# Feed-forward networks in two halves of inner features, with nine of 22 blocks as seven products of quarters

## The chip, the cores and the metric

One core of a Trainium2 chip runs the whole program. Its engines work side by side, each through its own queue in order: TensorE (PE, with its weight loads shown as PEld), VectorE (DVE), ScalarE (ACT), GpSimd (POOL) and SyncE (SP), which issues nearly all transfers. The metric is the device time of one execution in microseconds (us); lower is better.

## The reference, cut to what matters

The program runs a small sequence model: 512 tokens of 1,024 features pass two blocks with a mixer and two feed-forward networks each, and then further mixers on a longer sequence. The change touches the four feed-forward networks of the first part. Each computes, with 2,816 inner features:

```
def rmsnorm(x, g, eps=NORM_EPS):
    x32 = x.astype(jnp.float32)
    y = x32 * lax.rsqrt(jnp.mean(x32 * x32, axis=-1, keepdims=True) + eps)
    return (y * g.astype(jnp.float32)).astype(x.dtype)

def swiglu(h, w_up, w_down):
    gate, up = jnp.split(h @ w_up, 2, axis=-1)
    return (jax.nn.silu(gate) * up) @ w_down
```

and half of the result is added to x. All of it is in fp32.

## The kernel before, in words

**Layout.** Features lie on the 128 partitions and the 512 tokens along the free axis, so x is 8 tiles of 128x512 and the inner features are 22 blocks of 128. Block j has a gate and an up block of weights; each is one piece of 128x1024 (8 chunks of 128x128, half a megabyte) that SP fetches by one transfer.

**fp32 by three products.** TensorE takes each fp32 operand as two fp32r numbers, a high and a low part. `split` makes them: ScalarE copies the high part (L212), VectorE subtracts it from the source (L215; L206 and L209 are its forms with a scale or a bias). `mm3` (L227 to L231) then issues three matmuls, high x high, low x high and high x low. A gate or up block is 8 chunks x 3 = 24 matmuls of 512 columns, a pair 48. `weights` (L217) holds three buffers for a raw piece (`wraw`) and three pairs for its parts (`whi`, `wlo`). `bank` gives out four PSUM banks (`mm`).

**One network** (`ffn_body`, L318). The high and low parts of x are `hh` and `hl`, 8 tiles each. The reciprocal root of the mean square (`rbc`, copied from PSUM by L302) comes during the first pair. For each of 22 blocks j: 48 matmuls into two banks; VectorE multiplies the gate by `rbc` (L337), ScalarE takes silu (L338), VectorE multiplies up by `rbc` (L339), multiplies both (L340), and `split` leaves the result as `ah`, `al` (one pair of tiles for each j). Then the down projection: for each of 8 output blocks 22 chunks of weights in three pieces (1024, 1024 and 768 columns), 66 matmuls, and L346 adds half of the result to x.

**Work that is threaded through.** `extra` is a generator; `next(extra)` runs one step of it after each pair and after each down block, 30 times a network. The first two networks have none. The third carries `modulation(0)`, 24 steps: a step fetches a piece of `mod_w` into a `wraw` buffer and accumulates two halves of it, on VectorE into `acc` (L780), on ScalarE and GpSimd into `sq` (L781, L782); every fourth step ends an output of the modulation (two splits, four matmuls L792, L795, transposes, L799). The fourth network carries `context_in` (5 steps, 256-column work, tiles `ci`) and then `modulation(1)` (24 steps). After the fourth network `first_out` squares the 8 tiles of x on ScalarE (L727) and sums them on VectorE (L724, L728, L729) in the tiles `acc`, `sq` and `rbc`; `acc` and `sq` have one buffer each and are the same tiles as in modulation. The matmuls L262 with `ones` follow from its `acc`, and nothing of the next layer's normalised input exists before them. The next mixer's `ci` matmuls do not need them.

**Order.** A scheduling layer orders each engine's queue from the program text and puts in the semaphore waits; the queues then run in that fixed order.

## Time and profile before

| | |
|---|---|
| median of 3 runs | 3098.17 us (3096.71 to 3101.39) |
| the profiled execution | 3100.21 us, span 3098.5 us |
| TensorE busy | 3021.2 us, 98% |
| TensorE weight loads | 2519.9 us, 81% |
| VectorE busy | 1952.0 us, 63% |
| ScalarE busy | 1343.7 us, 43% |
| GpSimd busy | 451.6 us, 15% |
| granted TensorE clock | 9 tenths or more in each of 40 slices |

The span is what the program takes between its first and last instruction; the 1.7 us between it and the profiled time lie around it. Busy shares are means over the whole program, in which the four networks take about 1,460 us (60 to 422, 584 to 943, 943 to 1313 and 1640 to 2010 us).

### The profile page before, as it was taken

How to read it: one execution, taken by the hardware profiler on the slowest of the kernel's cores; microseconds unless marked ns; L12 is line 12 of the kernel's file. 1: busy time of each engine (PE TensorE's matmuls, PEld its weight loads, DVE VectorE, ACT ScalarE, POOL GpSimd, SP SyncE). 2: the span in 40 equal slices, each digit the busy share in tenths (PEclk: the TensorE clock that was granted, in tenths of full speed). 3: DMA queues.
4: the chain of work that ended last, by engine and by line, in shares of the span. 5: the costliest groups of instructions: out<-in, count | busy, mean ns of one | idle time of the engine just before them, and what ended most of it. 6: DMA issues, size and time to landing. Idle time of an engine off the chain costs nothing. (4 is left out here: it accounts for less than half of the span.)

```text
span 3098.5 us, 39749 instructions
## 1 busy us (share of the span) xinstructions
PE 3021.2 (98%) x15210; PEld 2519.9 (81%) x15210; DVE 1952.0 (63%) x3051; ACT 1343.7 (43%) x2359; POOL 451.6 (15%) x300
## 2 busy tenths in 40 slices
PE   8999999999999999999999999999999999999998
PEld 7888888888888888878788888878888887987776
DVE  6444357444436665377747665488778887668885
ACT  5332234322224443345535443346545643456663
POOL 0000000000002221023300221114334430001110
PEclk9999999999999999999999999999999999999999
DMA  6333322333334444312133444434344434531112
GB/s 205 95 97 92 100 86 78 101 96 100 92 100 130 132 148 127 98 56 62 54 88 124 136 143 133 146 96 137 111 125 147 137 111 156 173 103 38 37 54 92
DMA packets 112927, 335.84 MB, mean 108 GB/s; under 512 B 13512, under 2 KB 22984, under 8 KB 112736
## 3 DMA queue, kind: packets, MB, share of 16 engines
q1 hardware_dynamic: 112736, 333.30, 34.8%
q8 instruction: 119, 1.95, 0.3%
q14 instruction: 72, 0.59, 0.1%
HBM read 321.25 MB, written 11.96 MB: 108 GB/s over the span
## 5 line engine op out<-in xcount | busy, mean ns | idle before, releaser
L229 PE MATMUL mm<-hh,whi 128*128 128x512 f32 x2312 | 913.7, 395 | 6.5 <-DVE bt L1085 2.8
L230 PE MATMUL mm<-hl,whi 128*128 128x512 f32 x2312 | 905.1, 391 | 0.5 <-DVE hl L209 0.5
L231 PE MATMUL mm<-hh,wlo 128*128 128x512 f32 x2312 | 904.9, 391 | 0.0
L212 ACT ACTIVATE whi<-wraw 128x1024 fp32r<-128x1024 f32 (+3 forms) x458 | 462.0, 1012 | 953.0 <-PE mm L230 638.0
L215 DVE TENSOR_TENSOR wlo<-wraw,whi 128x1024 fp32r<-128x1024 f32 (+3 forms) x413 | 496.5, 1203 | 312.2 <-ACT whi L212 307.0
L229 PEld LDWEIGHTS mm<-hh,whi 128*128 128x128 f32 x2312 | 435.3, 188 | 96.7 <-DVE bt L1085 3.2
L231 PEld LDWEIGHTS mm<-hh,wlo 128*128 128x128 f32 x2312 | 435.5, 188 | 91.7 <-issue 1.0
L230 PEld LDWEIGHTS mm<-hl,whi 128*128 128x128 f32 x2312 | 435.5, 188 | 85.5 <-DVE hl L209 0.9
L229 PE MATMUL mm<-ah,whi 128*128 128x512 f32 x704 | 274.2, 390 | 0.0
L231 PE MATMUL mm<-ah,wlo 128*128 128x512 f32 x704 | 273.9, 389 | 0.0
L230 PE MATMUL mm<-al,whi 128*128 128x512 f32 x704 | 273.9, 389 | 0.0
L215 POOL TENSOR_TENSOR wlo<-wraw,whi 128x1024 fp32r<-128x1024 f32 (+1 forms) x69 | 168.7, 2445 | 393.6 <-ACT whi L212 246.0
L782 POOL TENSOR_TENSOR sq<-sq,wraw 128x512 f32<-128x512 f32 x84 | 122.3, 1456 | 437.3 <-ACT wraw L781 432.3
L339 DVE TENSOR_TENSOR fu<-mm,rbc 128x512 f32<-128x512 f32 x88 | 60.6, 689 | 185.8 <-PE mm L231 185.6
L229 PE MATMUL mm<-ci,whi 128*128 128x256 f32 (+1 forms) x552 | 166.5, 303 | 11.0 <-DVE bt L1085 5.0
L266 POOL TENSOR_TENSOR rs_r<-rs_v,neghalf 128x4 f32<-128x4 f32 (+1 forms) x23 | 25.4, 1104 | 1038.2 <-DVE rs_v L265 1038.2
L231 PE MATMUL mm<-ci,wlo 128*128 128x256 f32 (+1 forms) x552 | 164.6, 298 | 0.7 <-POOL wlo L215 0.7
L229 PEld LDWEIGHTS mm<-ah,whi 128*128 128x128 f32 x704 | 132.1, 188 | 27.6
L230 PEld LDWEIGHTS mm<-al,whi 128*128 128x128 f32 x704 | 132.1, 188 | 27.5
L231 PEld LDWEIGHTS mm<-ah,wlo 128*128 128x128 f32 x704 | 132.1, 188 | 27.5
L1197 ACT ACTIVATE lb<-lb,nbias 128x128 f32<-128x128 f32 x384 | 119.7, 392 | 35.1 <-POOL lb L1194 35.0
L230 PE MATMUL mm<-ci,whi 128*128 128x256 f32 x464 | 134.7, 290 | 0.0
(500 smaller groups left out, 4741.9 us busy)
## 6 DMA issues: line engine op xcount, KB each, us to landing
wraw<-w_up SPq DMA_DIRECT2D x176, 512.0 KB
wraw<-w_down SPq DMA_DIRECT2D x64, 512.0 KB
wraw<-mod_w SPq DMA_DIRECT2D x48, 512.0 KB
wraw<-m_in SPq DMA_DIRECT2D x48, 512.0 KB
lb<-cum_scr SPq DMA_DIRECT2D x64, 384.0 KB
wraw<-w_down SPq DMA_DIRECT2D x32, 384.0 KB
wraw<-diff_qkv SPq DMA_DIRECT2D x24, 512.0 KB
el<-ecum_scr SPq DMA_DIRECT2D x64, 192.0 KB
```

The lines of the kernel that those rows point to most:

```text
L212: nc.scalar.activation(hi, src, AF.Copy)
L215: (rest or nc.vector).tensor_tensor(lo, src, hv, op=ALU.subtract)
L229: mm(ps, ah, bh, start=start, stop=False)
L230: mm(ps, ah, bl, start=False, stop=False)
L231: self.last_mm = mm(ps, al, bh, start=False, stop=stop)
L266: nc.gpsimd.tensor_tensor(r[:, :nb], v[:, :nb], self.neghalf[:, :nb], op=ALU.pow)
L339: nc.vector.tensor_tensor(u, pu, rbc(), op=ALU.mult)
L782: nc.gpsimd.tensor_tensor(acc[1], acc[1], w, op=ALU.add)
L1197: nc.scalar.activation(w[dr][:, c], w[dr][:, c], AF.Exp, bias=nbias[:, c, dr * 32 + h : dr * 32 + h + 1])
```

## The change

The inner features are taken in two halves of 11 blocks: only 11 pairs `ah`, `al` are kept, and the down projection runs twice, each time over 11 chunks (pieces of 1024 and 384 columns) with an addition to x (L360 of the changed kernel). That frees the room for sums of the input. In every second block from j = 4 (4, 6, ... 20; nine in a network, 36 in all) the pair is done by `ffn_seven`. It views weights and input as 2 x 2 quarters (gate and up by two halves of the input features; input features by two halves of the tokens) and forms seven products of quarters, each 4 chunks x 3 = 12 matmuls of 256 columns: 84 matmuls of 256 columns in place of 48 of 512. For it VectorE makes four combinations of weight quarters (L396, L397, L400, L403) and their low parts (three of 1024 columns, one of 512), and puts the products together in seven operations of 256 columns (L425 to L437), followed by two multiplications by `rbc` of 512 (L434, L438). `ffn_sums` makes the four sums of input quarters, a quarter of them in each of the first four blocks: 4 operations of 256 columns (L375 to L378), and 4 splits of 256 columns. `next(extra)` is called in the 13 ordinary blocks and in the 16 passes of the down projection: 29 times a network. The fourth network's extra work has 29 steps, so its last step now runs behind the last pass of the down projection.

```diff
+            a2 = [(fp.tile([P, S], F32R, name=f"ah{j}"), fp.tile([P, S], F32R, name=f"al{j}")) for j in range(n)]
...
             for j in range(NFF):
...
+                t = u = None
+                if j >= 4 and j % 2 == 0:
+                    t, u = self.ffn_seven(fp, up[2 * j], up[2 * j + 1], hh, hl, sums, rbc)
+                else:
+                    pg, pu = self.bank(), self.bank()
+                    self.dense(up[2 * j], [(pg, hh, hl)])
+                    self.dense(up[2 * j + 1], [(pu, hh, hl)], within=rbc.start if j == 0 else None)
...
+                    next(extra, None)
                 nc.vector.tensor_tensor(u, t, u, op=ALU.mult)
-                self.split(u, ah[j], al[j])
-                next(extra, None)
-            for m in range(KC):
-                ps = self.bank()
-                self.dense(down[m], [(ps, ah, al)])
-                nc.vector.scalar_tensor_tensor(self.x[m], ps, 0.5, self.x[m], op0=ALU.mult, op1=ALU.add)
-                next(extra, None)
+                self.split(u, ah[j % n], al[j % n])
+                if j < 4:
+                    self.ffn_sums(fp, j, g, sums)
+                if j % n == n - 1:
+                    at = (j // n) * n * P
+                    for m in range(KC):
+                        ps = self.bank()
+                        self.dense(down[m][:, at : at + n * P], [(ps, ah, al)])
+                        nc.vector.scalar_tensor_tensor(self.x[m], ps, 0.5, self.x[m], op0=ALU.mult, op1=ALU.add)
+                        next(extra, None)
...
+        y = fp.tile([P, S], F32, name="fg", bufs=2)
+        nc.scalar.activation(y, z, AF.Copy, scale=gz)
+        w = fp.tile([P, S], F32, name="fu", bufs=2)
+        nc.vector.scalar_tensor_tensor(w[:, h0], x[:, h1], gx, y[:, h1], op0=ALU.mult, op1=ALU.add)
+        nc.vector.scalar_tensor_tensor(w[:, h1], x[:, h0], gx, w[:, h0], op0=ALU.mult, op1=ALU.subtract)
+        nc.vector.tensor_tensor(y[:, h0], y[:, h0], w[:, h1], op=ALU.add)
+        nc.vector.tensor_tensor(y[:, h1], x[:, h0], x[:, h1], op=ALU.subtract)
+        for q, (src, scale) in enumerate(((w[:, h0], None), (w[:, h1], -1.0), (y[:, h1], gx), (y[:, h0], None))):
+            self.split(src, sums[q][c][:, h0], sums[q][c][:, h1], scale=scale)
...
+        gh, gl = pair()
+        self.split(wg, gh, gl)
+
+        nc.vector.tensor_tensor(wt[:, b1], wu[:, b0], wg[:, b0], op=ALU.subtract)
+        nc.vector.tensor_tensor(wt[:, b0], wu[:, b1], wt[:, b1], op=ALU.subtract)
+        th, tl = pair()
+        self.split(wt, th, tl)
+        nc.vector.tensor_tensor(wu[:, b0], wu[:, b1], wu[:, b0], op=ALU.subtract)
+        uh, ul = pair()
+        self.split(wu, uh, ul)
+        nc.vector.tensor_tensor(wg[:, b1], wt[:, b0], wg[:, b1], op=ALU.subtract)
...
+        product(pa[:, h0], gh, gl, 0, quarter(0, h0))
+        nc.scalar.activation(v[:, h0], pa[:, h0], AF.Copy)
+        product(pb[:, h0], th, tl, 0, total(1))
+        product(pa[:, h1], gh, gl, 512, quarter(4, h0))
+        tt(t[:, h0], pa[:, h1], v[:, h0], op=ALU.add)
+        tt(v[:, h0], pb[:, h0], v[:, h0], op=ALU.add)
+        product(pc[:, h0], th, tl, 512, total(0))
+        tt(v[:, h1], pc[:, h0], v[:, h0], op=ALU.add)
+        product(pb[:, h1], uh, ul, 0, total(2))
+        tt(v[:, h0], pb[:, h1], v[:, h0], op=ALU.add)
+        tt(u[:, h1], pc[:, h0], v[:, h0], op=ALU.add)
+        product(pc[:, h1], vh, vl, 0, quarter(4, h1))
+        tt(t[:, h1], v[:, h0], pc[:, h1], op=ALU.subtract)
+        tt(t, t, r, op=ALU.mult)
+        nc.scalar.activation(t, t, AF.Silu)
+        product(pd[:, h0], uh, ul, 512, total(3))
+        tt(u[:, h0], pd[:, h0], v[:, h1], op=ALU.add)
+        tt(u, u, r, op=ALU.mult)
```

The scheduling layer's order decides what stands ahead of what. Three places of VectorE's queue follow. The first is in the third network, where pairs run with modulation's steps (L780 before, L869 in the changed kernel). Before, an ordinary block reads:

```order
L339 TENSOR_TENSOR fu<-mm,rbc 128x512
L780 SCALAR_TENSOR_TENSOR acc<-wraw,silu_c,acc 128x512
L340 TENSOR_TENSOR fu<-fg,fu 128x512
L215 TENSOR_TENSOR wlo<-wraw,whi 128x1024
L215 TENSOR_TENSOR al_6768<-fu,ah_6746 128x512
L780 SCALAR_TENSOR_TENSOR acc<-wraw,silu_c,acc 128x512
L337 TENSOR_TENSOR fg<-mm,rbc 128x512
L215 TENSOR_TENSOR wlo<-wraw,whi 128x1024
```

In the changed kernel a block of seven products has there the operations that put products together, between the low parts of the next weights:

```order
L425 TENSOR_TENSOR fg<-mm,fv 128x256
L426 TENSOR_TENSOR fv<-mm,fv 128x256
L215 TENSOR_TENSOR wlo<-wraw,whi 128x1024
L428 TENSOR_TENSOR fv<-mm,fv 128x256
L215 TENSOR_TENSOR wlo<-wraw,whi 128x1024
L430 TENSOR_TENSOR fv<-mm,fv 128x256
L869 SCALAR_TENSOR_TENSOR acc<-wraw,silu_c,acc 128x512
L431 TENSOR_TENSOR fu<-mm,fv 128x256
L437 TENSOR_TENSOR fu<-mm,fv 128x256
L869 SCALAR_TENSOR_TENSOR acc<-wraw,silu_c,acc 128x512
L438 TENSOR_TENSOR fu<-fu,rbc 128x512
```

L431 stands behind two low parts, L428, L430 and one step of modulation. The matmuls of the product `pc[:, h1]`, which write the bank that L431 reads, wait for it; on TensorE they stand among the first matmuls of the next block.

The second place is the start of the third network, block j = 2, where the changed kernel has:

```order
L215 TENSOR_TENSOR wlo<-wraw,whi 128x1024 x2
L349 TENSOR_TENSOR fu<-mm,rbc 128x512
L375 SCALAR_TENSOR_TENSOR fu<-x_92,cols,fg 128x256
L351 TENSOR_TENSOR fu<-fg,fu 128x512
L376 SCALAR_TENSOR_TENSOR fu<-x_92,cols,fu 128x256
L378 TENSOR_TENSOR fg<-x_92 128x256
L377 TENSOR_TENSOR fg<-fg,fu 128x256
L215 TENSOR_TENSOR al_8058<-fu,ah_8057 128x512
L215 TENSOR_TENSOR s_8077<-fu,s_8077 128x256
L206 SCALAR_TENSOR_TENSOR s_8081<-fu,s_8081 128x256
L206 SCALAR_TENSOR_TENSOR s_8085<-fg,cols,s_8085 128x256
L215 TENSOR_TENSOR s_8089<-fg,s_8089 128x256
```

The eight rows of 128x256 (L375 to L378, and the four splits into tiles s) are new in this block and stand between the ordinary ones.

The third place is the end of the fourth network. Before, VectorE has the sixth of the eight additions to x, the end of modulation (L795, L799), and then the first sums of squares:

```order
L346 SCALAR_TENSOR_TENSOR x_96<-mm,x_96 128x512
L215 TENSOR_TENSOR wlo<-wraw,whi 128x1024
L795 TENSOR_TENSOR acc<-aux,sq 2x512
L215 TENSOR_TENSOR wlo<-wraw,whi 128x768
L799 COPY mod_12974<-aux 128x8
L724 TENSOR_SCALAR acc<-rbc,fo_ge 128x512
L728 SCALAR_TENSOR_TENSOR acc<-sq,fo_ge,acc 128x512
L729 TENSOR_TENSOR rbc<-rbc,sq 128x512
```

In the changed kernel the end of modulation stands behind the last addition to x (L360 into x_97, the eighth tile), and the sums of squares behind that:

```order
L360 SCALAR_TENSOR_TENSOR x_97<-mm,x_97 128x512
L215 TENSOR_TENSOR wlo<-wraw,whi 128x1024
L884 TENSOR_TENSOR acc<-aux,sq 2x512
L215 TENSOR_TENSOR wlo<-wraw,whi 128x1024
L888 COPY mod_15259<-aux 128x8
L813 TENSOR_SCALAR acc<-rbc,fo_ge 128x512
L817 SCALAR_TENSOR_TENSOR acc<-sq,fo_ge,acc 128x512
L818 TENSOR_TENSOR rbc<-rbc,sq 128x512
```

L884 and L888 are L795 and L799 of before; L813, L817 and L818 are L724, L728 and L729. All of them moved behind the end of the down projection.

## Rows read from the trace of the kernel before

**Rows 1.** The page: busy time, share and instructions of each engine.
```profile
PE 3021.2 (98%) x15210; PEld 2519.9 (81%) x15210; DVE 1952.0 (63%) x3051; ACT 1343.7 (43%) x2359; POOL 451.6 (15%) x300
```
**Rows 2.** Stretches: length, busy PE, PEld, DVE, ACT, POOL, granted clock, DMA share, GB/s.
```profile
80.00:290.00 210.00, 210.00 (x928) 173.88 (x927) 96.72 (x115) 62.52 (x77) 0.00 (x0) 1.00 0.32 97
...
970.00:1190.00 220.00, 220.00 (x979) 178.79 (x978) 150.93 (x183) 97.05 (x131) 49.45 (x35) 1.00 0.46 143
...
1665.00:1885.00 220.00, 219.48 (x978) 178.84 (x977) 146.56 (x187) 93.19 (x128) 41.95 (x30) 1.00 0.43 136
```
**Rows 3.** Timeline of PE, first network: start, us, matmul; 48 apart.
```profile
90.23 0.39 PE L229 MATMUL mm<-hh,whi 128*128 128x512 f32 x1
...
101.11 0.39 PE L229 MATMUL mm<-hh,whi 128*128 128x512 f32 x1
```
**Rows 4.** Timeline of PE, matmuls of 256 columns; 41 apart.
```profile
2690.97 0.28 PE L229 MATMUL mm<-ci,whi 128*128 128x256 f32 x1
...
2695.89 0.28 PE L231 MATMUL mm<-yc,wlo 128*128 128x256 f32 x1
```
**Rows 5.** Groups of DVE, 80 to 290 us: count, busy, mean ns, idle before, releaser.
```profile
L215 DVE TENSOR_TENSOR wlo<-wraw,whi 128x1024 fp32r<-128x1024 f32 x39 | 47.6, 1221 | 4.8 <-ACT whi L212 4.8
L340 DVE TENSOR_TENSOR fu<-fg,fu 128x512 f32<-128x512 f32 x19 | 13.2, 692 | 2.0
...
L339 DVE TENSOR_TENSOR fu<-mm,rbc 128x512 f32<-128x512 f32 x19 | 13.1, 692 | 62.4 <-PE mm L231 62.4
```
**Rows 6.** Groups of DVE, 970 to 1190 us.
```profile
L215 DVE TENSOR_TENSOR wlo<-wraw,whi 128x1024 fp32r<-128x1024 f32 x40 | 54.2, 1356 | 13.1 <-ACT whi L212 13.1
L780 DVE SCALAR_TENSOR_TENSOR acc<-wraw,silu_c,acc 128x512 f32<-128x512 f32 x36 | 28.0, 777 | 25.7 <-DMA wraw<-mod_w 25.2
...
L340 DVE TENSOR_TENSOR fu<-fg,fu 128x512 f32<-128x512 f32 x20 | 18.6, 929 | 1.0
```
**Rows 7.** Groups of DVE by form, 256 columns.
```profile
L1164 DVE TENSOR_TENSOR yo<-aux,el 128x256 f32<-128x256 f32 x48 | 19.8, 416 | 0.3
```
**Rows 8.** Timeline of DVE and POOL, third network.
```profile
1053.92 2.67 POOL L782 TENSOR_TENSOR sq<-sq,wraw 128x512 f32<-128x512 f32 x2 [5.47 <-ACT wraw L781]
...
1055.56 2.11 DVE L215 TENSOR_TENSOR wlo<-wraw,whi 128x1024 fp32r<-128x1024 f32 x1 [1.14 <-ACT whi L212]
```
**Rows 9.** Timeline of DVE, start of the first network.
```profile
75.20 0.69 DVE L337 TENSOR_TENSOR fg<-mm,rbc 128x512 f32<-128x512 f32 x1
75.81 0.68 DVE L339 TENSOR_TENSOR fu<-mm,rbc 128x512 f32<-128x512 f32 x1
```
**Rows 10.** Timeline of PE, third network: the second pair's first matmul.
```profile
955.96 0.47 PE L229 MATMUL mm<-hh,whi 128*128 128x512 f32 x1
```
**Rows 11.** Timeline of DVE, end of the fourth network.
```profile
1996.31 0.67 DVE L795 TENSOR_TENSOR acc<-aux,sq 2x512 f32<-2x512 f32 x1
...
1997.86 0.47 DVE L724 TENSOR_SCALAR acc<-rbc,fo_ge 128x512 f32<-128x512 f32 x1
...
2014.65 0.75 DVE L728 SCALAR_TENSOR_TENSOR acc<-sq,fo_ge,acc 128x512 f32<-128x512 f32 x1 [0.76 <-ACT sq L727]
```
**Rows 12.** Timeline of ACT, the same stretch.
```profile
1999.88 0.63 ACT L727 ACTIVATE sq<-x 128x512 f32<-128x512 f32 x1 [2.23 <-DVE rbc L729]
...
2001.99 0.63 ACT L727 ACTIVATE sq<-x 128x512 f32<-128x512 f32 x1
```
**Rows 13.** Timeline of PE, the same stretch.
```profile
1994.10 0.40 PE L792 MATMUL aux<-whi,sel 128*2 128x512 f32 x1
...
2010.57 0.28 PE L229 MATMUL mm<-ci,whi 128*128 128x256 f32 x1
...
2016.32 0.95 PE L262 MATMUL aux<-ones,acc 128*128 128x1 f32 x8
```
**Rows 14.** Timeline of PE near the program's start, matmuls of 256 columns.
```profile
27.59 0.41 PE L231 MATMUL mm<-mh,wlo 128*128 128x256 f32 x1
27.80 0.41 PE L229 MATMUL mm<-mh,whi 128*128 128x256 f32 x1
```

More of the change, by code (lines that the diff above doesn't have):

```diff
@@ L327, in ffn_body @@
         up, down = self.d["w_up"][2 * i + s], self.d["w_down"][2 * i + s]
+        n = NFF // 2
         with self.pool("ffn") as fp:
-            ah = [fp.tile([P, S], F32R, name=f"ah{j}") for j in range(NFF)]
-            al = [fp.tile([P, S], F32R, name=f"al{j}") for j in range(NFF)]
+            a2 = [(fp.tile([P, S], F32R, name=f"ah{j}"), fp.tile([P, S], F32R, name=f"al{j}")) for j in range(n)]
+            ah, al = [a for a, _ in a2], [a for _, a in a2]
+            sums = [[fp.tile([P, S], F32R, name=f"s{q}{c}") for c in range(4)] for q in range(4)]
@@ L350, in ffn_body, with ffn_sums @@
         self.tap(f"ffn{i}{s}", self.x)
+    def ffn_sums(self, fp, c, g, sums):
+        nc = self.nc
+        x, z = self.x[c], self.x[c + 4]
+        gx, gz = self.col("norm_g", g + c), self.col("norm_g", g + c + 4)
+        h0, h1 = slice(0, S // 2), slice(S // 2, S)
+        y = fp.tile([P, S], F32, name="fg", bufs=2)
[7 more added lines that the diff above has]
+            self.split(src, sums[q][c][:, h0], sums[q][c][:, h1], scale=scale)
@@ new lines, in ffn_seven, with product @@
+    def ffn_seven(self, fp, gate, up, hh, hl, sums, rbc):
+        nc = self.nc
+        H = S // 2
+        h0, h1 = slice(0, H), slice(H, S)
+        b0, b1 = slice(0, 512), slice(512, 1024)
+        raw = lambda: self.wr.tile([P, 1024], F32, name="wraw")
+        pair = lambda: (self.wh.tile([P, 1024], F32R, name="whi"), self.wh.tile([P, 1024], F32R, name="wlo"))
+        wg, wu, wt = raw(), raw(), raw()
+        nc.sync.dma_start(wg, gate)
+        nc.sync.dma_start(wu, up)
+        gh, gl = pair()
[8 more added lines that the diff above has]
+        nc.vector.tensor_tensor(wg[:, b1], wt[:, b0], wg[:, b1], op=ALU.subtract)
+        vh = fp.tile([P, 512], F32R, name="w4h")
+        vl = fp.tile([P, 512], F32R, name="w4l")
+        self.split(wg[:, b1], vh, vl)
+        pa, pb, pc, pd = [self.bank() for _ in range(4)]
+        def product(ps, wh, wl, at, xs):
+            for c, (xh, xl) in enumerate(xs):
+                sl = slice(at + c * P, at + (c + 1) * P)
+                self.mm3(ps, wh[:, sl], wl[:, sl], xh, xl, c == 0, c == 3)
+        quarter = lambda c0, h: [(hh[c][:, h], hl[c][:, h]) for c in range(c0, c0 + 4)]
+        total = lambda q: [(t[:, h0], t[:, h1]) for t in sums[q]]
+        t = fp.tile([P, S], F32, name="fg", bufs=2)
+        u = fp.tile([P, S], F32, name="fu", bufs=2)
+        v = fp.tile([P, S], F32, name="fv", bufs=1)
+        r = rbc()
+        tt = nc.vector.tensor_tensor
+        product(pa[:, h0], gh, gl, 0, quarter(0, h0))
[12 more added lines that the diff above has]
+        tt(t, t, r, op=ALU.mult)
+        nc.scalar.activation(t, t, AF.Silu)
+        product(pd[:, h0], uh, ul, 512, total(3))
+        tt(u[:, h0], pd[:, h0], v[:, h1], op=ALU.add)
+        tt(u, u, r, op=ALU.mult)
+        return t, u
```

12 lines of the change are left out of this document (4 added, 8 removed).

## The prediction

> **What bounds the kernel now.** I read the page's busy times first: TensorE is busy for 98% of the span [rows 1]. Next come the stretches of the pairs: TensorE is busy for all of each at the full granted clock, while VectorE has 97 of 210 us in the first network, 151 of 220 in the third and 147 of 220 in the fourth [rows 2]. So there the time is TensorE's count of matmuls times their spacing, and the question is how much of VectorE's slack is spent. The groups of VectorE say what the slack is made of: in the first network it idles before L339 because it waits for TensorE [rows 5]; in the third the same operations take longer [rows 6].
>
> A bound for any change is the uncovered part of a chain: from 1994 to 2016 us the last step of modulation, the sums of squares and the `ones` matmuls run beside the end of the down projection, and TensorE has only the `ci` matmuls left to cover what is late there [rows 11 to 13].
>
> **Term 1, the products.** 48 matmuls of 512 columns take 101.11 - 90.23 = 10.88 us, 0.2267 each [rows 3]. The trace has the new form elsewhere: 256 columns, each with its own weights, 41 intervals in 4.92 us, 0.120 each [rows 4]. 84 x 0.120 = 10.08. A seven gains 0.80 us, 36 of them 28.8 us. (An eighth of the multiplications is worth 10.88 / 8 = 1.36 us; a half of 0.2267 is 0.1133, so 6.7 ns for each of 84 take back 0.56.) I take the whole 28.8, since the form is the same.
>
> The Trainium skill ("TensorE: Matmul & The Clock Gate", Back-to-back issue gap) gives an isolated gap of N/2.4 + 2.5 ns at the full clock, 109 and 216 ns for these two sizes, which would make term 1 about 43 us. Both rows lie above it (120 and 227), and the measured pair decides.
>
> **What VectorE must do now.** Prices: low part of 1024, 1.22; 512 columns, 0.69 [rows 5]; 256 columns, 0.42 [rows 7], with the scaled form unseen in the rows shown, bounded by 0.42 and 0.69 and taken at 0.48. Operations that need not wait start 0.08 us before the one ahead ends (75.81 against 75.20 + 0.69) [rows 9]. An ordinary block is 2 x 1.22 + 4 x 0.69 = 5.2 us. A seven is 3 x 1.22 (low parts of 1024) + 5 x 0.69 (four combinations, the low part of 512) + 7 x 0.42 (putting together) + 4 x 0.69 (two scalings by `rbc`, L351, `al`) = 12.8. A pair of blocks is 18.0 us against TensorE's 10.08 + 10.88 = 20.96, 86%. In networks three and four a pair of blocks also carries one step of modulation, 2 x 0.78 plus the steps' ends, 2.1 us, and GpSimd's operations lengthen VectorE's: 2.11 against 1.22 where an L782 runs [rows 8], and by the means of [rows 5] and [rows 6], (1.356 - 1.221) x 40 + (0.929 - 0.692) x 20 and as much again for `al`, some 15 us over 35 of them, 0.43 each. That is 21 to 22 us against 20.96: no slack. Where they meet the price is 0.9 (2.11 - 1.22), up to 1.33 (half of 2.67, which is two of them) [rows 8]; so before about half of them miss, and a VectorE that never idles would make fewer miss (first rival).
>
> The Trainium skill ("SBUF — State Buffer", SBUF: two separate sides) calls VectorE's and GpSimd's port pair an exclusive lock on which an operation with two SBUF inputs waits out the whole GpSimd instruction. By it every meeting costs what is left of the GpSimd instruction, which the +0.9 agrees with; if every one of the 46 below met so, the sum would be some 20 us higher.
>
> **Term 2, the seventh product.** `pc[:, h1]` writes the bank that L431 still reads. TensorE reaches it after six products and two matmuls of the next block, at 6 x 1.44 + 2 x 0.227 = 9.09 us from the block's start. The second weight pair comes free with the fourth product at 5.76; ScalarE's copy of 1024 columns lies between 0.63, its time for 512 [rows 12], and twice that, I take 1.05; the low part 1.22, L430 and L431 0.42 each; 8.87, and with some 0.4 for five hand-overs (an estimate) about 9.3. Late by about 0.25 in networks one and two. In three and four an L869 stands between, 0.66 more, of which I take 0.2, as it is not there every time: 0.45. 16 x 0.25 + 16 x 0.45 = 11 us (the first seven of each network is in term 3). Bounds: 0 if the hand-overs vanish, 0.9 each (29 us) if the L869 is always there.
>
> **Term 3, the first seven of each network.** The sums come in the first four blocks, and all of them are needed in block 4. From the first L337 to block 4 lie about 31 us: in the first network 75.20 to 106.2, in the third 957.98 to 955.96 + 3 x 10.88 = 988.6 [rows 9, 10]. VectorE has in that time, in the third network's new order: 16 operations of 512 on the ordinary blocks, 7 low parts, 32 operations of 256 for the sums (4 x 3.6 us), 4 combinations and 8 us of modulation: 11.0 + 8.5 + 14.4 + 2.8 + 8 = 44.7, less 0.08 at most of the starts, 41 to 43. The last low part may end 4.3 us into the seven, as it serves the fourth product. 42.5 - 30.6 - 4.3 = 7.6; with the collisions up to 11. In the first two networks there is no modulation, about 34 less overlaps, 1.3 late each by the queue's order; in the fourth `context_in` stands in for modulation with 256-column work, 4.5. Together 1.3 + 1.3 + 8 to 11 + 4.5, I take 18. Bounds 3 and 25.
>
> **Term 4, the pieces that end an output.** Every fourth step of modulation ends an output with two low parts of 512, L795 [rows 11] and copies, 2 x 0.69 + 0.67 + 0.25 = 2.3 us more on a VectorE without slack. The 13 steps of a network's ordinary blocks bring about three, six in both networks, one of them counted in term 3 and one behind the last seven: four times 2.1, 8.5 us (0 to 14).
>
> **Term 5, the end of network four.** Before, modulation's last matmuls ran at 1994.10, L795 at 1996.31, the sums of squares from 1997.86 to 2014.65 in steps of 2.11 us [rows 11, 12], since `acc` and `sq` have one buffer each; `ones` followed at 2016.32, 5.75 us behind the end of the down projection at 2010.57, filled by 48 `ci` matmuls x 0.120 = 5.8 us [rows 13]. Now that last step stands behind the last L360. Its four matmuls start when the down projection ends (call it T); L884 at T + 2.2, L813 at T + 3.8. Only then do the tiles come free; the first L817 comes 0.6 later, six steps of 2.11 to the last, and its 0.75: `ones` at T + 17.8. TensorE's 5.75 us of `ci` are the same: 12 us more of idling, plus the clock: behind idling the trace shows the 1.2 GHz level, 0.21 for 256 columns [rows 14], 0.09 more than at 2.4 GHz, on some 24 matmuls 2 us; less 1.3 of modulation's matmuls that move. 13 us (10 to 17).
>
> **At nothing.** The down projection in two passes of 33 matmuls, 7.48 us each: VectorE's addition, two low parts of 1024 and 384 columns come to 2.5 us a pass, and the transfers are the same bytes in 16 issues more; ScalarE's copies likewise. Without that cover a pass would cost its 0.69 addition, 22 us over 32. A seven takes all three raw buffers, so on SP's queue the next block's two transfers wait behind L403 and the 512 low part, and behind them the following seven's. The DMA engines are busy for 0.32 to 0.46 of the time [rows 2], so a piece that is issued has room; it is wanted a block later. If that cover is gone, the low parts of term 2 come later still, which its upper bound holds.
>
> **Sum.** -28.8 + 11 + 18 + 8.5 + 13 = +21.7. Against the profiled 3100.2 that is 3121.9. The median lies 2.0 below the profiled execution, so the median would be 3120.
>
> **Rivals.** *VectorE becomes the bound and every GpSimd operation blocks it* for 1.0 to 1.3 us instead of 0.43: some 46 of them run beside the pairs, 46 x 0.6 = 27 us at most, half of it in stretches without slack: 3135 to 3150. For it: [rows 8]. Against: before, half missed.
>
> *The waits are mostly covered*, because TensorE's four banks let the next block run ahead: terms 2 to 4 halve (19), term 5 stays: 3098.2 - 28.8 + 19 + 13 = 3101; 3094 to 3104, about no change. Against: the queue is in order and the seventh product stands among the next block's first matmuls.
>
> *The other side, faster:* VectorE keeps up at block 4 and in the sevens. It decides at one point: if the 42.5 us of work ahead of the third network's first seven shrinks to 35, terms 3 and 4 go, term 2 is a few us. 28.8 - 13 - 5 = 11 gained, 3087. Against: the prices are measured and the overlap of 0.08 is already in.
>
> *The weights' loads do not hide behind a matmul of 256 columns.* A load takes 2519.9 us / 15210 = 166 ns on the mean [rows 1], the matmul 120; 46 ns x 84 x 36 = 139 us, about 3260. The stretch of [rows 4] runs at 120 with such loads, so it has 1 in 100. The Trainium skill (the same page, The mechanism) says that a load overlaps a running matmul only where the row groups differ, which speaks for this rival; the trace disagrees.
>
> **How the numbers follow.** Forecast 0.62; blocked by GpSimd 0.17; covered 0.10; faster 0.10; loads 0.01. The forecast's own range is 3108 to 3134: of the bounds of terms 2 to 5, which don't all lie at one end, about a third to either side. The range for 8 in 10 takes in the covered case's upper part and half of the blocked one: 3101 to 3143. A difference under 0.2% (6 us) can hardly be told from none here: faster, below 3092, 0.10; the same, 3092 to 3104, 0.10 (the covered case); slower 0.80.
>
> **What would show it.** Matmuls of 256 columns at 0.120 us in the sevens (term 1). TensorE idle before a matmul with `w4h` behind L431, 0.2 to 0.5 us (term 2). A gap of several us before or in the first seven of the third network, with VectorE busy without a pause from 958 us (term 3). About 12 us of idle TensorE before the `ones` matmuls behind network four, and lower clock after it (term 5). VectorE near 100% in the pairs of networks three and four. Wrong would be: no idle TensorE in those pairs, or a spacing other than 0.120.

## The result, and the profile after

The changed kernel takes 3130.97 us (median of 4 runs, 3127.68 to 3131.66) against 3098.16 before (3096.71 to 3101.39): 32.8 us more, a ratio of 1.0106 (95% interval 1.0094 to 1.0118). The forecast was 3120, slower, in a range of 3101 to 3143: sign and range hold, the size was a third short. The terms behind it fared worse than their sum. The page of the changed kernel, busy time by engine, against [rows 1]:

```profile
span 3126.0 us, 43465 instructions
PE 3012.6 (96%) x16506; PEld 2565.7 (82%) x16506; DVE 2259.8 (72%) x3711; ACT 1455.9 (47%) x2579; POOL 463.8 (15%) x300
```

TensorE is busy for 8.6 us less and the span is 27.5 longer, so TensorE idles. Where it idles, the first `ones` matmul of each norm tells, ahead of and behind each network (timeline of TensorE; the second to last row is context's norm, early in network four, the last is network four's end):

```profile
67.73 0.95 PE L262 MATMUL aux<-ones,acc 128*128 128x1 f32 x8
418.35 0.95 PE L262 MATMUL aux<-ones,acc 128*128 128x1 f32 x8
584.48 0.95 PE L262 MATMUL aux<-ones,acc 128*128 128x1 f32 x8
940.79 0.95 PE L262 MATMUL aux<-ones,acc 128*128 128x1 f32 x8
1320.67 1.05 PE L262 MATMUL aux<-ones,acc 128*128 128x1 f32 x8
1676.71 0.50 PE L262 MATMUL aux<-ones,acc 128*128 128x1 f32 x4
2047.39 1.86 PE L262 MATMUL aux<-ones,acc 128*128 128x1 f32 x8 [10.85 <-DVE acc L817]
```

Before, the same matmuls started at 69.30, 425.09, 591.23, 952.16, 1316.93, 1673.35 and 2016.32 us (the last in [rows 13]). From norm to norm the first network takes 350.6 us in place of 355.8, the second 356.3 in place of 360.9, the third 379.9 in place of 364.8; from 1673.35 to the end 343.0 became 370.7. So: -5.2, -4.6, +15.1, +27.7. **The two networks without threaded work gained, the two with it lost.** The four differences add up to 33.0. That the two profiled executions differ by only 27.5 comes from outside the networks: from network four's `ones` to the end the traces take 1082.2 us before, 1078.6 here and 1075.8 in e1, whose program is that of before there. The stretches of the changed kernel (length, then busy PE, PEld, DVE, ACT, POOL, granted clock, DMA share, GB/s) show how. The first row is network one's first eleven blocks; then come, in networks three and four, blocks 0 to 10, eight passes, blocks 11 to 21, eight passes; the last is the end of network four:

```profile
72.00:178.00 106.00, 106.00 (x624) 94.07 (x624) 86.43 (x144) 48.34 (x73) 0.00 (x0) 1.00 0.29 92
...
944.00:1062.00 118.00, 112.91 (x644) 99.23 (x643) 105.64 (x165) 61.03 (x92) 21.27 (x13) 0.97 0.35 115
1062.00:1132.00 70.00, 66.92 (x281) 52.35 (x280) 40.28 (x50) 24.91 (x36) 20.81 (x14) 0.95 0.39 130
1132.00:1257.00 125.00, 121.22 (x728) 107.92 (x727) 105.90 (x157) 57.83 (x77) 18.17 (x12) 0.99 0.38 126
1257.00:1317.00 60.00, 60.00 (x267) 49.00 (x266) 35.03 (x46) 24.93 (x36) 6.02 (x5) 1.00 0.40 125
1654.00:1770.00 116.00, 112.30 (x647) 99.36 (x647) 102.73 (x175) 59.64 (x92) 8.32 (x5) 0.98 0.34 113
1770.00:1837.00 67.00, 64.51 (x277) 50.15 (x276) 40.45 (x48) 24.75 (x36) 20.53 (x13) 0.97 0.40 136
1837.00:1960.00 123.00, 120.12 (x726) 105.87 (x725) 103.67 (x151) 56.21 (x75) 19.44 (x11) 1.00 0.39 126
1960.00:2023.00 63.00, 61.02 (x271) 49.17 (x270) 35.12 (x46) 23.61 (x35) 19.00 (x13) 1.00 0.55 174
2023.00:2056.00 33.00, 19.38 (x104) 17.58 (x104) 19.20 (x31) 9.40 (x14) 2.76 (x3) 0.69 0.23 77
```

In these blocks of network one VectorE is at 82% and TensorE doesn't wait. Network three idles 5.1 + 3.1 + 3.8 = 12.0 us and then loses to the clock: in each of these three stretches it stands for some us at the lower of its two levels (1.2 GHz), and a mean of 0.97 over 118 us, 0.95 over 70 and 0.99 over 125 is at most 3.5 + 3.5 + 1.3 = 8.3 us of work not done. With about 6 us gained by nine sevens, 20.3 - 6 = 14, near the measured 15.1.

What TensorE waits for (line and what it waited for: us, times, longest), in blocks 0 to 10 of network three:

```profile
PE mm L231 <- DVE wlo L215: 3.3, 2, 2.2
PE aux L881 <- DVE wlo L215: 1.5, 1, 1.5
...
```

in its first eight passes, and in blocks 11 to 21:

```profile
PE aux L881 <- ACT whi L212: 1.9, 2, 1.4
PE aux L881 <- DVE wlo L215: 0.7, 2, 0.3
...
```

```profile
PE aux L484 <- DVE acc L884: 3.8, 2, 3.1
```

L881 (L792 before) and L484 are the four matmuls and the transposes that end an output of modulation. So most of the waiting, 7.9 of 12.0 us, is not before the sevens' own matmuls but before modulation's, in the passes too. One such pass, in order of time (SP's queue, VectorE, ScalarE, GpSimd, TensorE):

```profile
1092.28 1.91 POOL L871 TENSOR_TENSOR sq<-sq,wraw 128x512 f32<-128x512 f32 x1 [0.32 <-ACT wraw L870]
...
1094.22 0.33 SPq L862 DMA_DIRECT2D wraw<-mod_w  x1
...
1098.03 1.54 DVE L869 SCALAR_TENSOR_TENSOR acc<-wraw,silu_c,acc 128x512 f32<-128x512 f32 x2 [2.83 <-DMA wraw<-mod_w]
1098.87 1.47 ACT L870 ACTIVATE wraw<-wraw,silu_c 128x512 f32<-128x512 f32 x2 [6.31 <-DVE acc L869]
1099.67 3.03 POOL L871 TENSOR_TENSOR sq<-sq,wraw 128x512 f32<-128x512 f32 x2 [5.48 <-ACT wraw L870]
...
1102.73 0.33 SPq L862 DMA_DIRECT2D wraw<-mod_w  x1
1102.73 0.63 ACT L212 ACTIVATE whi<-sq 128x512 fp32r<-128x512 f32 x1 [1.88 <-POOL sq L871]
...
1103.41 0.40 PE L881 MATMUL aux<-whi,sel 128*2 128x512 f32 x1 [1.39 <-ACT whi L212]
```

SP issues a step's transfer just when GpSimd has read the piece before out of its raw buffer (1092.28 + 1.91 = 1094.19, issued at 1094.22; 1099.67 + 3.03 = 1102.70, issued at 1102.73). From issue to issue a step takes 8.5 us here, the shortest time of these eight passes, and a pass of 33 matmuls takes 7.48.

### The profile page after: what moved, and what is told of

It is laid out like the page before. It is cut to its first block, busy times and chain, and to the rows that moved or that the text cites. A ratio compares the mean times of both kernels' runs of the same rounds, so it can differ in the third digit from the quotient of the medians.

```text
span 3126.0 us, 43465 instructions
## 1 busy us (share of the span) xinstructions
PE 3012.6 (96%) x16506; PEld 2565.7 (82%) x16506; DVE 2259.8 (72%) x3711; ACT 1455.9 (47%) x2579; POOL 463.8 (15%) x300
## 5 line engine op out<-in xcount | busy, mean ns | idle before, releaser
L212 ACT ACTIVATE whi<-wraw 128x1024 fp32r<-128x1024 f32 (+4 forms) x526 | 507.0, 966 | 753.5 <-PE mm L230 562.0
L229 PE MATMUL mm<-hh,whi 128*128 128x512 f32 (+1 forms) x2024 | 770.2, 381 | 8.3 <-DVE bt L1174 2.8
L231 PE MATMUL mm<-hh,wlo 128*128 128x512 f32 (+1 forms) x2024 | 762.4, 377 | 1.1 <-DVE wlo L215 1.1
L230 PE MATMUL mm<-hl,whi 128*128 128x512 f32 (+1 forms) x2024 | 761.9, 376 | 0.5 <-DVE hl L209 0.5
L215 DVE TENSOR_TENSOR wlo<-wraw,whi 128x1024 fp32r<-128x1024 f32 (+4 forms) x481 | 544.5, 1134 | 233.8 <-ACT whi L212 223.5
L229 PEld LDWEIGHTS mm<-hh,whi 128*128 128x128 f32 x2024 | 382.2, 189 | 75.7 <-DVE bt L1174 3.2
L231 PEld LDWEIGHTS mm<-hh,wlo 128*128 128x128 f32 x2024 | 382.2, 189 | 69.1 <-DVE wlo L215 1.5
L230 PEld LDWEIGHTS mm<-hl,whi 128*128 128x128 f32 x2024 | 382.3, 189 | 63.7 <-DVE hl L209 0.9
L229 PE MATMUL mm<-ah,whi 128*128 128x512 f32 x704 | 275.6, 392 | 0.0
L871 POOL TENSOR_TENSOR sq<-sq,wraw 128x512 f32<-128x512 f32 x84 | 134.1, 1596 | 542.9 <-ACT wraw L870 533.6
L229 PE MATMUL mm<-ci,whi 128*128 128x256 f32 (+1 forms) x552 | 167.3, 304 | 10.2 <-DVE bt L1174 5.0
L231 PE MATMUL mm<-s,wlo 128*128 128x256 f32 x576 | 164.6, 288 | 4.8 <-DVE wlo L215 4.8
L229 PE MATMUL mm<-s,whi 128*128 128x256 f32 x576 | 165.6, 288 | 1.2 <-DVE fv L426 1.2
L230 PE MATMUL mm<-s,whi 128*128 128x256 f32 x576 | 164.5, 286 | 0.0
L229 PEld LDWEIGHTS mm<-ah,whi 128*128 128x128 f32 x704 | 133.1, 189 | 28.1 <-ACT ah L212 0.2
```

The source lines that it names most:

```text
L212: nc.scalar.activation(hi, src, AF.Copy)
L215: (rest or nc.vector).tensor_tensor(lo, src, hv, op=ALU.subtract)
L229: mm(ps, ah, bh, start=start, stop=False)
L230: mm(ps, ah, bl, start=False, stop=False)
L231: self.last_mm = mm(ps, al, bh, start=False, stop=stop)
L871: nc.gpsimd.tensor_tensor(acc[1], acc[1], w, op=ALU.add)
```

## The experiments

All ratios are to the kernel before on the same chip. Time from norm to norm of each network against before, in us, is read as above (networks three and four from their own norm, before 364.8 and 369.1):

| kernel | median, us (before) | ratio, 95% | net 1 | net 2 | net 3 | net 4 and end |
|---|---|---|---|---|---|---|
| changed | 3130.97 (3098.16) | 1.0106, 1.0094 to 1.0118 | -5.2 | -4.6 | +15.1 | +27.7 |
| e1_first_two | 3085.48 (3096.32) | 0.9963, 0.9951 to 0.9976 | -5.2 | -4.7 | 0.0 | 0.0 |
| e2_even_steps | 3130.47 (3096.32) | 1.0110, 1.0097 to 1.0124 | -5.2 | -4.7 | +23.9 | +21.0 |
| e3_halves | 3138.36 (3096.32) | 1.0136, 1.0122 to 1.0149 | 0.0 | 0.0 | +10.0 | +29.4 |
| e4_two_steps | 3121.76 (3096.32) | 1.0075, 1.0060 to 1.0090 | -5.2 | -4.6 | +12.7 | +21.0 |
| e5_no_gpsimd | 3099.90 (3096.56) | 1.0014, 1.0005 to 1.0023 | -5.2 | -4.6 | +0.3 | +10.0 |
| e6_early_sums | 3112.34 (3096.56) | 1.0053, 1.0039 to 1.0067 | -5.2 | -4.7 | +15.7 | +17.4 |
| e7_from_six | 3115.44 (3096.56) | 1.0057, 1.0042 to 1.0073 | -5.2 | -4.6 | +7.5 | +18.9 |
| e8_every_third | 3088.28 (3096.56) | 0.9974, 0.9964 to 0.9984 | -5.2 | -4.6 | +0.7 | 0.0 |
| e9_own_tile | 3111.10 (3095.60) | 1.0053, 1.0038 to 1.0069 | -5.2 | -4.6 | +8.0 | +15.4 |
| e10_combined | 3073.70 (3095.60) | 0.9929, 0.9916 to 0.9941 | -5.2 | -4.6 | -4.7 | -5.8 |
| e11_before_no_gpsimd | 3096.72 (3095.60) | 1.0006, 0.9997 to 1.0016 | 0.0 | 0.0 | +0.3 | 0.0 |

**e1_first_two**, the change in networks one and two alone (`ffn_whole` is the function of before):

```diff
-            self.ffn_body(i, s, extra)
+            (self.ffn_whole if i else self.ffn_body)(i, s, extra)
...
```

> The first two networks as changed (halves and sevens), the third and fourth as before. Theory A (the loss is in the threaded work of networks three and four, VectorE keeps up in the sevens): networks one and two keep the gain that the changed kernel's trace shows, 6.5 and 4.6 us, so 3098 - 11 = 3087 us. Theory B (the prediction's: the seventh product and the late first seven cost 3 to 4 us in each of these two): 3090 us. If the sevens gave nothing by themselves: 3098.

10.8 us are gained, as Theory A had it (the 6.5 us in it for network one are 5.2 from norm to norm). Sevens and halves are a gain of about 5 us in a network with nothing threaded through; the whole loss lies in networks three and four.

**e2_even_steps**, a step behind each of the 22 blocks and each second pass:

```diff
                 self.split(u, ah[j % n], al[j % n])
+                next(extra, None)
...
-                        next(extra, None)
+                        if m % 2:
+                            next(extra, None)
```

> The changed kernel with the steps of the threaded work spread as before: one behind each of the 22 blocks, the sevens too, and one behind every second pass of the down projection. Theory A (passes of 7.5 us are too short for a step's chain of transfer, VectorE, ScalarE, GpSimd and TensorE, and the last step comes too late): the idle time in the passes (about 8 us with the clock that falls behind it) and at the end of network four (20 us) goes, so about 3100 to 3105 us. Theory B (VectorE has no slack in the pairs of networks three and four): the end's 20 us go, but 18 more steps beside sevens cost 1 to 1.5 us each, so 3131 - 20 + 22 = about 3133 us, with TensorE idle before matmuls on w4h and on the sums.

Both theories are half right, and the time is nearly Theory B's. Here are its stretches, blocks 0 to 10 and the passes behind them in network three, and what TensorE waited for in the first of them:

```profile
944.00:1081.00 137.00, 123.27 (x688) 105.53 (x687) 120.40 (x183) 69.55 (x106) 33.35 (x22) 0.99 0.34 119
1081.00:1140.00 59.00, 59.00 (x264) 48.18 (x263) 31.40 (x38) 19.46 (x26) 10.15 (x8) 1.00 0.41 137
```

```profile
PE mm L231 <- DVE wlo L215: 4.2, 4, 2.3
PE mm L229 <- DVE fv L427: 2.9, 2, 1.6
PE mm L229 <- DVE fu L432: 2.8, 3, 1.2
PE aux L485 <- DVE acc L885: 1.9, 1, 1.9
...
```

With a step in every second pass the passes don't wait at all, and the end doesn't (Theory A); with a step beside each seven TensorE idles 13.7 us in these blocks, most of it before matmuls of sevens that wait for low parts and for two of the operations that put products together, L427 and L432 (L426 and L431 of the changed kernel). The waits for low parts are those of term 3 and the wait for L432 is that of term 2; L427 stands in no term. VectorE is at 88% there, so it isn't its sum of work alone that is late.

**e3_halves**, the halves and the changed places of the steps, no sevens and no sums:

```diff
-                if j >= 4 and j % 2 == 0:
+                if False:
...
-                    next(extra, None)
+                    if j < 4 or j % 2:
+                        next(extra, None)
...
-                if j < 4:
-                    self.ffn_sums(fp, j, g, sums)
```

> The two halves with their 16 passes and the steps of the threaded work where the changed kernel has them, but all blocks ordinary: no sevens, no sums. Theory A: VectorE has its slack back and still the passes and the end of network four lose what they lose in the changed kernel, and modulation's first end too in part: 3098 + 20 (end) + 8 (passes) = about 3126 us. Theory B: the passes cost nothing, the end 13 to 20: 3111 to 3118 us.

It is slower than the changed kernel, further out than Theory A said: most of the loss is there without VectorE's additional work. Networks one and two are as before to 0.1 us, so passes without steps cost nothing; three and four lose 39 us. The passes of network three, where VectorE is at 51%:

```profile
1081.00:1145.00 64.00, 60.71 (x253) 47.61 (x252) 32.67 (x39) 20.81 (x30) 19.79 (x13) 0.95 0.43 147
```

```profile
PE aux L879 <- ACT whi L212: 2.3, 2, 1.4
...
```

The same waits before modulation's matmuls, the same clock. Against this kernel the sevens cost 5 us in network three and win 2 in four.

**e4_two_steps**, two more steps in network four:

```diff
                     self.ffn_sums(fp, j, g, sums)
+                if i == 1 and s == 1 and j in (4, 6):
+                    next(extra, None)
```

> The changed kernel with two more steps in the fourth network, behind its sevens j = 4 and j = 6, so that the threaded work ends two passes earlier, about where it ended before. Both theories: the end of network four loses what it lost (20 us between the end of the down projection and the next layer's first matmul), so 3131 - 20 = 3111 us, less 1 to 3 us that the two steps may cost beside the sevens. If the sums of squares are late for another reason (the last addition to x): 3125 to 3131 us.

9.5 us better (ratio 1.0075 in place of 1.0106), half of what was expected. The end is near that of before (TensorE idles 5.0 us from 1975 to 2060), but blocks 0 to 10 of network four, which took the two steps, now idle 9.1 of 123 us where they idled 3.7 of 116: a step beside a seven is paid for. These 5.4 us are over half of what is missing; the rest stays open.

**e5_no_gpsimd**, modulation's second sum on VectorE:

```diff
-                        nc.scalar.activation(w, w, AF.Copy, scale=sc[:, kc, 1:2])
-                        nc.gpsimd.tensor_tensor(acc[1], acc[1], w, op=ALU.add)
+                        nc.vector.scalar_tensor_tensor(acc[1], w, sc[:, kc, 1:2], acc[1], op0=ALU.mult, op1=ALU.add)
```

> The changed kernel with the second half of each modulation step accumulated by VectorE too (84 operations of 512 columns, 0.75 us each, in place of ScalarE's multiplication and GpSimd's addition). Theory A (the chain transfer, VectorE, ScalarE, GpSimd, TensorE is too long for a pass of 7.5 us, and GpSimd lengthens VectorE's operations): TensorE's waits before modulation's matmuls shrink, about 10 us with the clock: 3120 us. Theory B (VectorE's load beside the sevens decides): 1.5 us more of VectorE in each of 26 ordinary blocks makes the pairs wait: 3131 + 20 = about 3150 us, with waits before w4h and the sevens' weights as in the kernel with evenly spread steps.

Theory B falls, and Theory A's size was a third of what came. VectorE does 84 operations more, ScalarE 84 fewer, and the kernel is some 28 us faster than the changed one (its ratio is lower by 0.0092). Blocks 0 to 10, the passes and blocks 11 to 21 of network three:

```profile
944.00:1062.00 118.00, 113.68 (x653) 99.65 (x652) 108.21 (x180) 52.19 (x78) 0.18 (x1) 0.99 0.34 115
1062.00:1132.00 70.00, 70.00 (x313) 56.61 (x312) 50.34 (x74) 20.75 (x28) 0.00 (x0) 1.00 0.47 152
1132.00:1250.00 118.00, 118.00 (x722) 105.10 (x721) 104.58 (x164) 48.91 (x64) 0.00 (x0) 1.00 0.39 131
```

TensorE waits neither in the passes nor in the later blocks, with VectorE at 89%; only the first sevens and the end still wait. What GpSimd did to VectorE shows in two groups of the changed kernel, blocks 0 to 10 of network three (count, busy, mean ns, idle before and its releaser):

```profile
L438 DVE TENSOR_TENSOR fu<-fu,rbc 128x512 f32<-128x512 f32 x4 | 6.0, 1510 | 0.0
...
L396 DVE TENSOR_TENSOR wraw<-wraw 128x512 f32<-128x512 f32 x4 | 2.8, 692 | 4.5 <-POOL sq L871 4.5
```

and in one of this kernel:

```profile
L438 DVE TENSOR_TENSOR fu<-fu,rbc 128x512 f32<-128x512 f32 x4 | 2.7, 683 | 0.0
```

A seven's first combination waits for GpSimd, since the third raw buffer that it writes still holds modulation's piece, and behind L396 stands all of VectorE. And L438 takes 0.83 us longer in the kernel in which GpSimd adds beside it. The Trainium skill ("SBUF — State Buffer", SBUF: two separate sides) has a lock that would do the latter; these rows agree with it. This run takes out ScalarE's 84 multiplications together with GpSimd's additions, so by itself it doesn't say which of the two cost the 28 us.

**e6_early_sums**, the sums of squares beside the last eight passes, in the tiles `fg` and `fu`:

```diff
                         next(extra, None)
+                        if i == 1 and s == 1 and j == NFF - 1:
+                            if m == 0:
+                                four = [fp.tile([P, S], F32, name=k, bufs=2) for k in ("fg", "fu", "fg", "fu")]
+                            self.early_sum(m, four)
...
+        nc.scalar.activation(sq, self.x[c], AF.Square)
+        nc.vector.scalar_tensor_tensor(acc, sq, self.ge[:, c : c + 1], t[0], op0=ALU.mult, op1=ALU.add)
+        nc.vector.tensor_tensor(one, t[1], sq, op=ALU.add)
...
```

> The changed kernel, with the sums of squares behind network four formed during the last eight passes in tiles of their own (free since the last block), only the last of eight steps in the shared tiles. If the chain of squares behind the shared tiles is the larger part of the end's loss (term 5): the matmuls with ones come about 12 to 14 us earlier, 3131 - 13 = 3118 us, and about 8 us of the end's loss remain (the last step's own chain of transfers, ScalarE, GpSimd and VectorE, and the low clock). If the last step's own chain is the larger part: 3125 us. If sums beside the passes delay the passes: 3131 or more.

About 16 us better by the medians (1.0053), 11 by the spans of the profiled executions (this run's lies 4.4 us above its median, the changed kernel's 3.3 below), 10 of them in network four's stretch. The single tiles and the chain of seven steps were the larger part of the end, 10 of its 19 us (term 5 below).

**e7_from_six**, sevens from j = 6 in networks three and four:

```diff
-                if j >= 4 and j % 2 == 0:
+                if j >= (6 if i else 4) and j % 2 == 0:
...
-                    next(extra, None)
+                    if j != 4:
+                        next(extra, None)
```

> The changed kernel with networks three and four starting their sevens at j = 6 in place of 4 (j = 4 ordinary, without a step, so that all other steps stay where they are). Term 3 as predicted (sums and combinations don't fit into the first four blocks beside modulation): the waits before the first seven's weights, 2.2 and 2.4 us, and the half clock behind them go, about 8 to 10 us less 1.4 for two sevens not done: 3123 us. If the waits move to j = 6, since VectorE has no slack to catch up: 3131 us.

Better than expected: 7.6 us in network three and 8.8 in four, with one seven less in each. Four blocks with the sums, the first combinations and modulation were too short for VectorE, and the wait doesn't move on to j = 6.

**e8_every_third**, networks one and two changed, four as before, three with five sevens and a step in every second pass:

```diff
-            self.ffn_body(i, s, extra)
+            (self.ffn_whole if i and s else self.ffn_body)(i, s, extra)
...
-                if j >= 4 and j % 2 == 0:
+                if (j in (7, 10, 13, 16, 19)) if i else (j >= 4 and j % 2 == 0):
...
-                        next(extra, None)
+                        if m % 2:
+                            next(extra, None)
...
```

> Networks one and two as changed, network four as before, network three with five sevens in every third block (j = 7, 10, 13, 16, 19), steps behind its 17 ordinary blocks and every second pass. Theory A and B both leave VectorE at about 92% there (12.8 + 2 x 7.3 + 2 of lengthening in 31.8 us): network three gains 5 x 0.7 = 3.5 us, 3085.5 - 3.5 = 3082 us. If even so its first seven and modulation's ends wait: 3086 to 3090 us.

A miss: network three loses 0.7 us where 3.5 were to be gained. TensorE idles 2.3 of 126 us in blocks 0 to 10, all of it in blocks 2 and 3, where the sums stand beside modulation, ahead of the first seven, and with GpSimd and the raw buffers as they were; where the rest of the 4.2 us went stays open.

**e9_own_tile**, GpSimd kept, ScalarE's product in a tile of its own:

```diff
+            self.fp = fp
...
-                        nc.scalar.activation(w, w, AF.Copy, scale=sc[:, kc, 1:2])
-                        nc.gpsimd.tensor_tensor(acc[1], acc[1], w, op=ALU.add)
+                        part = self.fp.tile([P, S], F32, name="mw", bufs=2)
+                        nc.scalar.activation(part, w, AF.Copy, scale=sc[:, kc, 1:2])
+                        nc.gpsimd.tensor_tensor(acc[1], acc[1], part, op=ALU.add)
```

> The changed kernel, ScalarE's product of each modulation step written into a tile of its own (two buffers) and not back into the raw weight buffer; GpSimd adds it as before. The raw buffer then comes free with ScalarE and not with GpSimd, all else is the same work. If the raw buffers are what costs (a seven takes all three, and its combination L396 waited 4.5 us for GpSimd's L871 in the first half of network three): most of the 29 us that the kernel without GpSimd gained, about 3108 us. If it is GpSimd's chain and its hold on VectorE's operations: 3125 to 3131 us.

Some 16 us (1.0053), over half of what e5 gained. The passes of network three, whose 70 us lost 3.1 to idling and 3.5 to the clock, are now full:

```profile
1062.00:1132.00 70.00, 69.61 (x316) 56.24 (x315) 50.55 (x62) 28.66 (x40) 24.16 (x15) 1.00 0.48 160
```

So in the passes it is the raw buffer that GpSimd keeps: a step's transfer is issued there every 6.0 to 6.5 us, but for the steps that end an output. The first blocks of network three still idle 5.8 us. Of the other 12 us of e5 the trace shows a part. In six sevens of network three and six of network four TensorE waits 0.33 to 0.39 us for L432 (L431 of the changed kernel), 4.3 us in all, where L870 stands ahead of it beside GpSimd's additions and takes 1.45 us in place of 0.74; in e5 such waits come to 0.7 us. One of the twelve (GpSimd, VectorE, TensorE):

```profile
1039.35 3.36 POOL L873 TENSOR_TENSOR sq<-sq,mw 128x512 f32<-128x512 f32 x2 [18.28 <-ACT mw L872]
1040.13 1.45 DVE L870 SCALAR_TENSOR_TENSOR acc<-wraw,silu_c,acc 128x512 f32<-128x512 f32 x1
1041.97 0.39 PE L229 MATMUL mm<-hh,w4h 128*128 128x256 f32 x1 [0.35 <-DVE fu L432]
```

So about a third of the 12 us is GpSimd's hold on VectorE's operations. What the rest is made of, the same hold in other places, GpSimd's share of the chain or ScalarE's multiplications, which e5 takes out too, these runs don't separate.

**e10_combined**, e5, e6 and e7 together, with a step behind the ordinary block j = 4:

```diff
+                        nc.vector.scalar_tensor_tensor(acc[1], w, sc[:, kc, 1:2], acc[1], op0=ALU.mult, op1=ALU.add)
...
+                            self.early_sum(m, four)
...
+                if j >= (6 if i else 4) and j % 2 == 0:
...
```

> The changed kernel with modulation on VectorE alone, the early sums of squares, and sevens from j = 6 in networks three and four (j = 4 ordinary and with a step, so the threaded work ends a pass earlier). If the three causes are separate: 3100 (without GpSimd) - 20 (end) - 7 (first sevens and the clock behind them) = about 3074 us, 22 below the kernel before. If VectorE, which carries all of it, becomes the bound: 3090 us.

As expected: 3073.7, 21.9 us below the kernel before, and networks three and four gain like one and two. The causes nearly add up: e5 and e7 gained 14.8 and 7.6 us in network three, which would leave -7.3 and left -4.7, and e5, e6 and e7 gained 17.7, 10.3 and 8.8 in four, which would leave -9.1 and left -5.8. Each run alone took away a little that another takes away too. That the expected parts (20 for the end, 7 for the first sevens) gave the total so well is in part luck. Blocks 0 to 10 of network three, and the stretch from network four's last passes to the next layer:

```profile
944.00:1062.00 118.00, 117.58 (x643) 100.94 (x643) 108.42 (x179) 53.82 (x81) 0.23 (x1) 1.00 0.37 128
...
1995.00:2030.00 35.00, 32.81 (x187) 28.19 (x186) 30.03 (x51) 14.86 (x22) 3.09 (x4) 1.00 0.14 49
```

**e11_before_no_gpsimd**, the kernel before with e5's edit:

```diff
-                        nc.gpsimd.tensor_tensor(acc[1], acc[1], w, op=ALU.add)
+                        nc.vector.scalar_tensor_tensor(acc[1], w, sc[:, kc, 1:2], acc[1], op0=ALU.mult, op1=ALU.add)
```

> The kernel before, with modulation on VectorE alone. TensorE is busy all through the networks before, so it gains nothing: 3096 to 3098 us. If GpSimd cost something there too: 3090 us.

No difference that can be told from none. What e5 takes away cost nothing before; the change made it cost.

## Why the prediction came out as it did

**Term 1** (28.8 us) is right in kind, somewhat large. The matmuls of 256 columns run at 0.120, but with the changes between sizes a pair of blocks takes 21.07 us (below), so a seven gains 0.69 and not 0.80, 25 us in all, 6.2 a network. Networks one and two show 5.2 and 4.6 of it (term 3). The same matmul of the seventh product, two pairs of blocks apart:

```profile
279.01 0.28 PE L230 MATMUL mm<-hl,w4h 128*128 128x256 f32 x1
...
321.14 0.28 PE L230 MATMUL mm<-hl,w4h 128*128 128x256 f32 x1
```

**Term 2** (11 us) failed. L431 is in time: in a seven of network one

```profile
134.16 0.42 DVE L431 TENSOR_TENSOR fu<-mm,fv 128x256 f32<-128x256 f32 x1
```

ends at 134.58, and the product that waits for it starts at 134.67. That seven begins at 125.57, so L431 was done after 9.01 us and not 9.3: the chain was priced rightly at 8.87, but of the 0.4 us charged for hand-overs only some 0.15 were there, and a margin of 0.1 us became a wait of 0.25 or 0.45, 32 times over. In networks three and four the L869 that was feared does stand there, in 12 of 18 sevens. But in ten of those the scheduling layer has put the product behind five matmuls of the next block and not behind two (the one at 1039.82 us, for example, with L431 done at 1039.58), and those three are worth the 0.7 us that L869 takes; in the other two a shorter low part (384 columns, 0.55 us, in place of 1024, 1.22) stands ahead of L430. TensorE waits for L431 in one seven of the 18, 0.85 us, and in one of network two, 0.1. With a step beside every seven (e2) or a longer L869 (e9) the wait does come, 2.8 us in three places and 4.3 in twelve.

**Term 3** (18 us) came out right in sum, in part by luck: starting two blocks later gives 7.6 and 8.8 us back (e7), and 0.7 more each for the seven not done, 17.8. The term gave networks three and four 8 to 11 and 4.5 us; a good third of what they lost is the low clock behind the waits, which it did not hold (5.1 us idle, 3.5 of clock in network three's first stretch). To networks one and two it gave 1.3 each, and there it failed: TensorE doesn't wait for their first seven at all (106.00 of 106.00 us above). What they fall short of 6.2, 1.0 and 1.6 us, has for 1.0 us in each another cause: behind the last pass the next layer's first matmul waits for the last addition to x, which before it did not, and so stands 1.27 us behind the matmul ahead of it and not 0.23, alike in both networks.

```profile
413.59 0.39 PE L231 MATMUL mm<-ah,wlo 128*128 128x512 f32 x1
414.86 0.47 PE L229 MATMUL mm<-hh,whi 128*128 128x512 f32 x1 [0.88 <-DVE x L360]
```

**Term 4** (8.5 us): TensorE did wait for modulation's ends in the blocks, 1.5 + 3.8 us in network three. But VectorE was not without slack: it is busy for 90 and 85% of those blocks. The waits come from the order of its queue together with the raw buffer. The split of an output stands behind a seven's L396, and L396 waits for GpSimd:

```profile
978.13 0.69 DVE L396 TENSOR_TENSOR wraw<-wraw 128x512 f32<-128x512 f32 x1 [2.19 <-POOL sq L871]
...
979.48 0.39 PE L881 MATMUL aux<-wlo,sel 128*2 128x512 f32 x1 [1.45 <-DVE wlo L215]
```

The longest wait, 3.1 us before L484 at 1147.79, is alike: L884, which it needs, stands at 1147.06 behind a seven's four combinations, and the first of them started at 1139.53, when GpSimd had let go of the buffer (1.18 us of waiting). Without GpSimd (e5) neither wait is there.

**At nothing** was the step that failed worst. The passes were priced by TensorE, VectorE's sum and the bytes, without threaded work, and that much e3 confirms in networks one and two. But a pass carries a step, as a down block of twice its length did before, and a step's chain with the release of its raw buffer takes 8.5 us against 7.48. Passes and the clock behind their waits cost 6.6 us in network three and, by the same sum (2.5 + 2.0 idle, 2.0 of clock), about as much in four. The term followed the release of the raw buffers for a seven (behind L403) and asked of the rest only whether the DMA engines had room; who releases the buffer of a step in a pass, GpSimd's L871, it did not ask.

**Term 5** (13 us) had the right chain and the wrong start. It took T + 2.2 for L884, but the last step's splits, two pieces of weights and the last L360 stand ahead. T is 2022.3 here, and L884 came at T + 7.0:

```profile
2029.34 0.67 DVE L884 TENSOR_TENSOR acc<-aux,sq 2x512 f32<-2x512 f32 x1
```

`ones` came at T + 25.1 and not T + 17.8. For part of that time the clock stands at the lower level (0.69 over the last stretch). The end cost 19 us to the `ones` matmuls (25.1 - 5.75); e6 gave back 10 of them in its trace.

The sum, -25 + 1 + 18 + 5 + 13 + 19 and 2 for the last addition in networks one and two, is +33, near the measured 32.8, though the parts overlap by a us or two (the 1.5 us of term 4 are in e7's gain too, and 0.8 us of the passes in the end). The forecast's +21.7 had some 10 too many in term 2 and 3 in term 4, and 13 too few in the passes, 6 at the end and 4 in term 1. That the time fell into the range is owed in part to these errors of either sign. Of the signs, the spacing of 0.120, the gap in the third network's first seven (2.2 us at its longest) and the idle time before `ones` came (10.9 us); the waits before `w4h` and a VectorE near 100% did not.

**The rivals.** GpSimd was the right name for the largest cause (28 us of 33 go without it and ScalarE's multiplications), but the mechanism given, its hold on VectorE's operations, was the smaller part: over half is the raw buffer (e9), and of the rest 4.3 us are seen to be the hold. "Mostly covered" and "faster" fell in networks three and four and hold in one and two. The loads of the weights do hide behind 256 columns, as [rows 4] had it. That rival's price was read too low, too: 166 ns is the loads' busy time shared out, in which overlapping loads count once; a single load takes 188 ns on the mean (L229 PEld before), which would have made it 206 us. The rule on row groups that is cited there stands in the Trainium skill ("TensorE: Matmul & The Clock Gate", The mechanism); [rows 4] disagree with it.

## What to carry to other kernels

When a loop is cut into shorter turns, whatever one turn carries along (a step of other work) must fit into the shorter turn as a chain from buffer release to last reader, not only as a sum of busy times. A ring of buffers is as slow as its slowest reader: here an addition on an engine that is busy for 15% of the span held the buffer that the next step's transfer and the next seven's first combination were waiting for. And a scheme that takes fewer multiplications pays only where the engines that it loads have nothing else to carry: first measure it where it stands alone (e1), then clear the other places one cause at a time (e5, e6, e7).
